# More buffers and other PSUM banks in a recurrence, one more probability buffer and sixfold softmax scalars in an attention

## The chip, the cores and the metric

The kernel runs on one core of a Trainium2 chip. Its time is the device time of one execution in microseconds (us). Five engines have an instruction stream of their own, each worked off in order: PE (TensorE, the matmuls), DVE (VectorE), ACT (ScalarE), POOL (GpSimd) and SP (SyncE, here only the issuer of DMAs). They meet through semaphores.

## The reference

A trunk of two layers on a residual stream of 1 x 1024 tokens x 1024 channels, all in float32. Each layer is a token mixer and then a gated MLP with a causal convolution.

```python
# layer 0, HGRN2, 8 heads of 128 keys and 128 values
forget = lb + (1 - lb) * sigmoid(f);  key_in = 1 - forget;  log_f = log(forget)
S_t = diag(exp(log_f_t)) S_{t-1} + k_t v_t^T;  o_t = S_t^T silu(q_t)
o = rmsnorm(o, out_norm) * silu(g);   x += o @ w_out
# layer 1, MLA, 8 heads: q and k of 128 + 64 (rotary) channels, v of 128
c_q, c_kv, k_rope = split(h @ w_in, [256, 512]);  q = rmsnorm(c_q) @ w_q_up;  k, v from rmsnorm(c_kv) @ w_kv_up
o = softmax(causal(rmsnorm(q) . rmsnorm(k) * scale)) @ v;   x += o @ w_out
# after each: conv_ffn
u = h @ w_up; y = conv3(u); gate, up = split(y); x += (silu(gate) * up) @ w_down     # width 2816
```

## The kernel before, in words

Channels lie on the partitions, tokens on the free axis, in two halves of 512 tokens (`hf`). Every float32 weight and activation of a projection is split into a high and a low part (`split`, L126 to 131: ACT casts the high part, POOL or DVE subtracts to get the low one). A product is three matmuls in the format fp32r (`acc3`, L147 to L149), and weights come 512 KB at a time by a DMA and `load_w` (tag "w", three slots). The recurrence, the transposes and the sums over tokens are plain float32 matmuls.

The kernel goes through the stages in this order: HGRN2, its output projection, FFN, MLA (its shared projections, then attention by heads), its output projection, FFN.

HGRN2 works on 16 units, a head `hd` and a half `hf` each. `project` makes F, K, q, Q, v and g of the next unit; `recur` does the recurrence of the present one. In `recur` seven score groups of 8 matmuls each (L406: once with q, then once before each of six levels) alternate with `scale`, in which DVE multiplies Q (L417) and POOL multiplies K (L419) by the products `tot` of one level. DVE puts each group into SD (L410, L429). An eighth group (`sc64`, L432) follows, ACT copies all to ST (L436 to L438), PE transposes K (`pT`, L443), ACT copies that back to K (L445), and then come for four chunks `po` (L451 and L453) and the update `pu` (L456), from which DVE or ACT makes the state (L461). `flip` transposes g (L478) and splits it, and DMAs write it away (`o_spill`); `out_projection` reads it back (`oall`).

Buffers come from pools: a tile has a tag, and the tag a number of buffers (`bufs`). In PSUM, the pool `g_ps` has two banks with tag "sc" for the score groups, sc64, pT and pu and one for po; the pool behind `ps_wo` has two banks with tag "wo" that only the first projection of the HGRN2 stage uses, and `ps_mm` has two banks for the projections. In MLA, `attend` (L694 to L757) takes for two blocks of 128 queries the scores `sp` (L710, three banks), the maximum (`mx`, `nb`), the exponential into `pp` with the sum `sm` (L725, ACT), the normalization in place (L730, ACT), transposes into `ps_wo` (L739), their split into th and tl, and the products with v (L751, L752).

The order of the instructions on each engine is not the order of the code. A scheduler puts it together while the program is built: it goes through the program with durations of its own, and picks for each engine among the instructions whose operands are ready and whose buffer is free. So a buffer more, or another bank, moves instructions far from the line that names it. On the chip the order is then fixed.

The lines that the change touches are these: the tiles Fg, K, Q and v of `project`; `sc` in `scores`, SD, tot and ST in `recur`; `mstage`; the pool `m_p` of MLA; mx, nb and sm in `attend`; and the load of the first half of the query weights, `wq`, before the first `clora`.

Of the kernel before, what the change touches and what calls it, by code (L numbers as in the profile page):

```python
# [9 lines left out]
F32 = mybir.dt.float32  # L10
# [9 lines left out]
P = 128  # L20
D = 1024
S = 1024
HF = 512
# [7 lines left out]
LEVELS = (1, 2, 4, 8, 16, 32)  # L31
# [27 lines left out]
def trunk_kernel(ctx: ExitStack, tc: tile.TileContext, x, pos, par, gout, cst, msk, w_hin, w_hout,  # L59
# [261 lines left out]
    def hgrn(layer, h):  # L321
        with ExitStack() as st:
# [28 lines left out]
            def project(hd, hf, bank=ps_mm):  # L351
                wf, wq, vgh, vgl = wts[hd]
                hh, hl, rb, y = h[hf]

                def proj(w):
                    p = bank()
                    acc3(p, [(w[0][:, k * P:(k + 1) * P], w[1][:, k * P:(k + 1) * P], hh[:, k, :], hl[:, k, :])
                             for k in range(KD)])
                    return p

                pf = proj(wf)
                Fg = early.tile([P, HF], F32, tag="F", name="Fg")
                K = tp.tile([P, HF], F32, tag="K", name="K")
                dve.tensor_tensor(out=Fg, in0=pf, in1=rb, op=ALU.mult)
                act.activation(out=K, in_=Fg, func=AF.Sigmoid, scale=-1.0)
                act.activation(out=Fg, in_=Fg, func=AF.Sigmoid)
                pool.tensor_scalar(out=Fg, in0=Fg, scalar1=oml[:, hd:hd + 1], scalar2=lb[:, hd:hd + 1],
                                   op0=ALU.mult, op1=ALU.add)
                pool.tensor_scalar(out=K, in0=K, scalar1=oml[:, hd:hd + 1], scalar2=0.0, op0=ALU.mult, op1=ALU.add)
                pq = proj(wq)  # L370
                q = early.tile([P, HF], F32, tag="q", name="q", bufs=1)
                Q = tp.tile([P, HF], F32, tag="Q", name="Q")
                dve.tensor_tensor(out=q, in0=pq, in1=rb, op=ALU.mult)  # L373
                act.activation(out=Q, in_=q, func=AF.Sigmoid)
                dve.tensor_tensor(out=q, in0=q, in1=Q, op=ALU.mult)
                dve.tensor_tensor(out=Q, in0=q, in1=Fg, op=ALU.mult)

                v = tp.tile([P, 4, P], F32, tag="v", name="v")
                g = tp.tile([P, 4, P], F32, tag="g", name="g", bufs=3)
                for tt in range(2):  # L380
                    pv = ps_mm()
                    for t2 in range(2):
                        t = 2 * tt + t2
                        ts_ = slice(t * P, (t + 1) * P)
                        acc3(pv[:, t2 * 256:(t2 + 1) * 256],
                             [(hh[:, k, ts_], hl[:, k, ts_], vgh[:, k, :], vgl[:, k, :]) for k in range(KD)])
                    p3 = v3(pv, 2)
                    for t2 in range(2):
                        t = 2 * tt + t2
                        yt = y[:, t:t + 1]  # L390
                        act.activation(out=v[:, t, :], in_=p3[:, t2, 0:P], func=AF.Identity, scale=yt)
                        act.activation(out=g[:, t, :], in_=p3[:, t2, P:2 * P], func=AF.Sigmoid, scale=yt)
                        dve.scalar_tensor_tensor(out=g[:, t, :], in0=p3[:, t2, P:2 * P], scalar=yt, in1=g[:, t, :],  # L393
                                                 op0=ALU.mult, op1=ALU.mult)
                pool.tensor_tensor(out=g, in0=g, in1=goutb[:, None, :].broadcast_to([P, 4, P]), op=ALU.mult)
                return Fg, K, q, Q, v, g

            def recur(hd, hf, prj, state):
                Fg, K, q, Q, v, g = prj

                def scores(qq):
                    sc = ps.tile([P, 4, 64], F32, tag="sc", name="sc", bufs=2)
                    for c in range(4):
                        for b in range(2):
                            sl = slice(c * P + b * 64, c * P + b * 64 + 64)
                            pe.matmul(sc[b * 64:b * 64 + 64, c, :], lhsT=K[:, sl], rhs=qq[:, sl], start=True, stop=True)  # L406
                    return sc

                SD = tp.tile([P, 4, 64], F32, tag="SD", name="SD", bufs=1)
                dve.tensor_tensor(out=SD, in0=scores(q), in1=fold[:, None, 0:64].broadcast_to([P, 4, 64]), op=ALU.mult)  # L410

                def scale(tot, m):
                    nb = HF // (2 * m)
                    tv = tot.rearrange("p (b two) -> p b two", two=2)
                    Qv = Q.rearrange("p (b two m) -> p b two m", two=2, m=m)
                    Kv = K.rearrange("p (b two m) -> p b two m", two=2, m=m)
                    dve.tensor_tensor(out=Qv[:, :, 1, :], in0=Qv[:, :, 1, :],  # L417
                                      in1=tv[:, :, 0:1].broadcast_to([P, nb, m]), op=ALU.mult)
                    pool.tensor_tensor(out=Kv[:, :, 0, :], in0=Kv[:, :, 0, :],  # L419
                                       in1=tv[:, :, 1:2].broadcast_to([P, nb, m]), op=ALU.mult)  # L420
                    nt = tp.tile([P, nb], F32, tag=f"tot{m}", name=f"tot{m}", bufs=2 if m == 64 else 1)
                    dve.tensor_tensor(out=nt, in0=tv[:, :, 0], in1=tv[:, :, 1], op=ALU.mult)
                    return nt

                tot = Fg
# [5 lines left out]
                for c in range(4):  # L431
                    pe.matmul(sc[0:64, c, :], lhsT=K[:, c * P:c * P + 64], rhs=Q[:, c * P + 64:(c + 1) * P],  # L432
                              start=True, stop=True)
                ST = tp.tile([P, 4, P], F32, tag="ST", name="ST", bufs=1)
                pool.memset(ST[64:P, :, 0:64], 0.0)
                act.copy(out=ST[0:64, :, 0:64], in_=SD[0:64])  # L436
                act.copy(out=ST[64:P, :, 64:P], in_=SD[64:P])
# [55 lines left out]
            goutb = wv.tile([P, P], F32, tag="goutb", name="goutb")  # L493
            nc.sync.dma_start(out=goutb, in_=gout.partition_broadcast(P))
            nc.sync.dma_start(out=cs, in_=cst)
            mstage = tp.tile([P, len(LEVELS), 64], F32, tag="ST", name="mstage", bufs=1)
            nc.sync.dma_start(out=mstage, in_=msk)
            dve.tensor_copy(out=masks, in_=mstage)
            prj = project(0, 0, ps_wo)
# [41 lines left out]
    def mla(h):  # L541
        with ExitStack() as st:
            tp = st.enter_context(tc.tile_pool(name="m_t", bufs=2))
            mp = st.enter_context(tc.tile_pool(name="m_c", bufs=1))
            pp_ = st.enter_context(tc.tile_pool(name="m_p", bufs=3))
            ps = st.enter_context(tc.tile_pool(name="m_ps", bufs=1, space=PSUM))
            krot = tp.tile([P, 2, HF], F32, tag="krot", name="krot", bufs=1)
            ckv = mp.tile([P, 2, 2, S], F32R, tag="ckv", name="ckv")
# [146 lines left out]
            def attend(hd, b, kk, vv, qq, rq, oh, ol):  # L695
                pts = []
                for j in (2 * b, 2 * b + 1):
# [1 line left out]
                    segs = [(0, max(w, 256))] if w <= HF else [(0, w // 2), (w // 2, w // 2)]  # L699
                    qs = slice((j % 4) * P, (j % 4 + 1) * P)  # L700
                    ns = len(segs)
                    mx = tp.tile([P, 2], F32, tag="mx", name="mx")
                    sps = []
                    for si, (c0, n) in enumerate(segs):
                        sp = ps_s()
# [7 lines left out]
                            pe.matmul(sp[:, d0:d0 + P], lhsT=identb, rhs=cmask, start=False, stop=True)  # L713
                        nv = min(n, w)
                        dve.tensor_reduce(out=mx[:, si:si + 1], in_=sp[:, 0:nv], op=ALU.max, axis=AX.X)
                    nb = tp.tile([P, 1], F32, tag="nb", name="nb")
                    if ns == 2:
                        dve.tensor_tensor(out=mx[:, 0:1], in0=mx[:, 0:1], in1=mx[:, 1:2], op=ALU.max)
                    rqj = rq[:, j % 4:j % 4 + 1]
                    dve.scalar_tensor_tensor(out=nb, in0=mx[:, 0:1], scalar=-1.0, in1=rqj, op0=ALU.mult, op1=ALU.mult)  # L720
                    pp = pp_.tile([P, S], F32, tag="p", name="pp")
                    sm = tp.tile([P, 2], F32, tag="sm", name="sm")
                    for si, (c0, n) in enumerate(segs):
                        nv = min(n, w)
                        act.activation(out=pp[:, c0:c0 + nv], in_=sps[si][:, 0:nv], func=AF.Exp, bias=nb, scale=rqj,  # L725
# [33 lines left out]

            wk = [load_w(w_min[2]), load_w(w_min[3])]  # L760
            wr = load_w(w_min[4])
            wq = [load_w(w_min[0], "wo", tp, 1)]
            raw = fetch_w(w_min[1])
            wq.append([pp_.tile([P, S], F32R, tag="p", name="wcq") for _ in range(2)])
            split(raw, *wq[1])
# [283 lines left out]
```

## Time and profile before

| what | us |
|---|---|
| median of 3 runs | 2585.41 |
| lowest and highest | 2581.57, 2588.17 |
| the profiled execution | 2581.05 |
| its span | 2579.2 |

The profiled execution stands 4.36 us under the median. The span goes from the first to the last instruction; 1.85 us lie around it. The stages, by the lines that run in them: HGRN2 up to about 545 us from the start of the span, its last unit and output projection to 650, FFN to 1351, MLA's shared projections to 1425, attention to about 1805, then the output projection and the second FFN.

The page gives for each engine the busy time, and for groups of instructions the idle time before them and which engine ended it. PE is busy in almost all of the span, so what matters is where it is idle, and what it does that is not needed.

### The profile page before, as it was taken

To read this page: it belongs to the slowest core of one execution; us is meant where nothing else is said; L and a number is where in the kernel's file an instruction comes from. 1 tells how busy PE (TensorE), PEld (TensorE's weight loads), DVE (VectorE), ACT (ScalarE), POOL (GpSimd) and SP (SyncE) were. 2 spreads that over 40 slices of the span, in tenths; PEclk is the share of its full clock that TensorE was granted. 3 is DMA by queue.
4 is the path that set the end of the run, shared out by engine and by line. 5 is a ranking of instruction groups with operands and counts; after the bars stand their busy time and mean duration, and the time that the engine had idled before them with its cause. 6 is when DMAs were issued, how large, how long until landed. Compare 5 with 4: busy or idle time off the path is not lost.

```text
span 2579.2 us, 35799 instructions
## 1 busy us (share of the span) xinstructions
PE 2483.0 (96%) x13860; PEld 2069.2 (80%) x13860; DVE 1698.1 (66%) x3033; ACT 1080.6 (42%) x1777; POOL 392.5 (15%) x386
## 2 busy tenths in 40 slices
PE   7999999998999999999999999999999999999999
PEld 6888888876777778888888788888877787888887
DVE  8355555555788888774535777777578888875333
ACT  5322223322444444433433566656444444443322
POOL 3334445521100000000003323221000000000000
PEclk9999999999999999999999999989999999999999
DMA  3111111343433332264331000002543333226443
GB/s 138 42 50 50 50 50 66 113 144 121 154 120 111 108 112 89 90 230 155 128 126 50 17 34 33 34 26 103 200 155 120 109 110 111 91 91 220 155 170 116
DMA packets 88298, 270.18 MB, mean 105 GB/s; under 512 B 9920, under 2 KB 10304, under 8 KB 86976
## 3 DMA queue, kind: packets, MB, share of 16 engines
q1 hardware_dynamic: 88128, 267.90, 29.5%
q8 instruction: 109, 1.79, 0.3%
q14 instruction: 61, 0.50, 0.1%
HBM read 207.04 MB, written 60.82 MB: 104 GB/s over the span
## 4 chain that ended last, share of the span: by engine, by line
PE 86%; DVE 6%; ACT 3%; DMA 3%; issue 1%; SPq 0%; ACTq 0%; DVEq 0%
PE ps_mm L251 19%; PE ps_up L251 9%; PE ps_mm L147 8%; PE ps_mm L149 8%; PE ps_mm L148 7%; PE ps_up L942 7%; PE ps_mm L942 5%; PE ps_wo L942 5%; PE ps_wo L251 3%; PE sp L710 3%; PE ps_misc L942 2%; PE sc L406 2%; PE ps_misc L167 2%; DMA open_spill<-part 1%; PE ps_wo L739 1%
## 5 line engine op out<-in xcount | busy, mean ns | idle before, releaser
L128 ACT CAST whi<-wraw 128x1024 fp32r<-128x1024 f32 (+1 forms) x328 | 321.3, 993 | 579.2 <-PE ps_misc L942 236.6
L131 DVE TENSOR_TENSOR wlo<-wraw,whi 128x1024 fp32r<-128x1024 f32 (+1 forms) x298 | 337.9, 1146 | 286.3 <-ACT whi L128 285.9
L251 PE MATMUL ps_mm<-bop,whi 128*128 128x512 f32 x1536 | 477.7, 393 | 17.3 <-ACT x L888 9.5
L251 PEld LDWEIGHTS ps_mm<-bop,whi 128*128 128x128 f32 x1536 | 285.9, 188 | 89.8 <-ACT x L888 15.4
L251 PE MATMUL ps_mm<-bop,wlo 128*128 128x512 f32 x768 | 296.4, 391 | 0.9 <-DVE wlo L131 0.9
L862 DVE SCALAR_TENSOR_TENSOR x<-x,prm,x 128x1023 f32<-128x1023 f32 (+1 forms) x176 | 223.5, 1279 | 48.9 <-ACT x L859 47.9
L251 PE MATMUL ps_up<-bop,whi 128*128 128x512 f32 x704 | 220.7, 394 | 0.9 <-ACT whi L128 0.9
L251 PEld LDWEIGHTS ps_mm<-bop,wlo 128*128 128x128 f32 x768 | 144.2, 188 | 33.6 <-DVE wlo L131 2.2
L942 PE MATMUL ps_up<-ring,whi 128*128 128x512 f32 x528 | 159.9, 389 | 0.0
L251 PEld LDWEIGHTS ps_up<-bop,whi 128*128 128x128 f32 x704 | 131.8, 188 | 33.1 <-ACT whi L128 2.6
L417 DVE TENSOR_TENSOR Q<-Q,tot 128x256 f32<-128x256 f32 x96 | 65.6, 683 | 133.2 <-PE sc L406 105.3
L147 PE MATMUL ps_mm<-vgh,hh 128*128 128x256 f32 x512 | 146.0, 285 | 5.9 <-DVE q L373 5.6
L149 PE MATMUL ps_mm<-vgh,hl 128*128 128x256 f32 x512 | 145.4, 284 | 0.0
L148 PE MATMUL ps_mm<-vgl,hh 128*128 128x256 f32 x512 | 143.8, 281 | 0.0
L859 ACT ACTIVATE x<-x,prm 128x1024 f32<-128x1024 f32 x88 | 109.3, 1243 | 70.0 <-DVE x L886 48.2
L251 PE MATMUL ps_up<-bop,wlo 128*128 128x512 f32 x352 | 138.5, 394 | 0.0
L845 DVE TENSOR_TENSOR wraw<-wraw 128x512 f32<-128x512 f32 x176 | 120.8, 686 | 2.2
L147 PE MATMUL ps_mm<-hh,whi 128*128 128x512 f32 x288 | 115.7, 402 | 2.2 <-DVE g L393 1.2
L710 PE MATMUL sp<-kk,qq 128*128 128x256 f32 (+4 forms) x480 | 109.1, 363 | 8.7 <-ACT pp L725 8.5
L942 PEld LDWEIGHTS ps_up<-ring,whi 128*128 128x128 f32 x528 | 99.2, 188 | 20.7
L149 PE MATMUL ps_mm<-hh,wlo 128*128 128x512 f32 x288 | 115.5, 401 | 0.0
L888 ACT COPY x<-ps_mm 128x512 f32<-128x512 f32 x84 | 49.1, 584 | 153.0 <-PE ps_mm L251 153.0
(296 smaller groups left out, 5544.3 us busy)
## 6 DMA issues: line engine op xcount, KB each, us to landing
wraw<-in_w_up_dram SPq DMA_DIRECT2D x104, 512.0 KB, 3.7
wraw<-in_w_down_dram SPq DMA_DIRECT2D x88, 512.0 KB, 3.5
act_spill<-x SPq DMA_DIRECT2D x44, 512.0 KB, 2.6
araw<-act_spill SPq DMA_DIRECT2D x88, 256.0 KB, 3.6
wraw<-in_w_hin_dram SPq DMA_DIRECT2D x38, 512.0 KB, 3.5
oall<-o_spill SPq DMA_DIRECT2D x64, 256.0 KB, 4.6
o_spill<-oh SPq DMA_DIRECT2D x32, 256.0 KB, 2.0
o_spill<-ol SPq DMA_DIRECT2D x32, 256.0 KB, 2.2
```

The source lines that it names most:

```text
L128: act.copy(out=hi, in_=src)
L131: lo_eng.tensor_tensor(out=lo, in0=src, in1=hi.bitcast(F32), op=ALU.subtract)
L147: pe.matmul(ps, lhsT=lh, rhs=rh, start=(i == 0), stop=False)
L148: pe.matmul(ps, lhsT=lh, rhs=rl, start=False, stop=False)
L149: pe.matmul(ps, lhsT=ll, rhs=rh, start=False, stop=(i == n - 1))
L251: pe.matmul(p, lhsT=a[l][:, ks], rhs=b[:, r, k, :], start=first and k == 0 and n == 0, stop=k == KH - 1 and n == 2, skip_group_check=not f ...
L417: dve.tensor_tensor(out=Qv[:, :, 1, :], in0=Qv[:, :, 1, :], in1=tv[:, :, 0:1].broadcast_to([P, nb, m]), op=ALU.mult)
L710: pe.matmul(sp[:, 0:n], lhsT=qq[:, a, qs], rhs=kk[:, c, cl], start=(i == 0), stop=last)
L845: dve.tensor_tensor(out=o, in0=p, in1=q, op=op)
L859: act.activation(out=y, in_=u, func=AF.Identity, scale=cw(2, ff), bias=pcol("cb", layer * 44 + ff))
L862: dve.scalar_tensor_tensor(out=y[:, i:S], in0=u[:, 0:S - i], scalar=cw(2 - i, ff), in1=y[:, i:S], op0=ALU.mult, op1=ALU.add)
L942: pe.matmul(acc[d], lhsT=w[l][:, d * P:(d + 1) * P], rhs=a[:, r], start=j == 0 and n == 0, stop=j == NFF - 1 and n == 2)
```

## The change

Of the recurrence: Fg, K, Q and v have three buffers where they had two; SD and ST have two where they had one; tot has two at every level where only the last had. The tile `sc` of the seven score groups of a unit goes from the pool `g_ps` (tag "sc", two banks, shared with sc64, pT and pu) to the pool of `ps_wo` (tag "wo", two banks). Of attention: `pp` has four buffers for three; mx, nb and sm have six for two. The weights `wq[0]` had a buffer of their own in the pool `m_t`; now they take one of the three slots of the tag "w", which wk[0], wk[1] and wr fill when it is loaded. No instruction is added and none taken away; each engine has as many as before.

```diff
@@ project
-                Fg = early.tile([P, HF], F32, tag="F", name="Fg")
-                K = tp.tile([P, HF], F32, tag="K", name="K")
+                Fg = early.tile([P, HF], F32, tag="F", name="Fg", bufs=3)
+                K = tp.tile([P, HF], F32, tag="K", name="K", bufs=3)
...
-                Q = tp.tile([P, HF], F32, tag="Q", name="Q")
+                Q = tp.tile([P, HF], F32, tag="Q", name="Q", bufs=3)
...
-                v = tp.tile([P, 4, P], F32, tag="v", name="v")
+                v = tp.tile([P, 4, P], F32, tag="v", name="v", bufs=3)
@@ recur
-                    sc = ps.tile([P, 4, 64], F32, tag="sc", name="sc", bufs=2)
+                    sc = psg.tile([P, 4, 64], F32, tag="wo", name="sc", padded_shape=[P, 8, 64])
...
-                SD = tp.tile([P, 4, 64], F32, tag="SD", name="SD", bufs=1)
+                SD = tp.tile([P, 4, 64], F32, tag="SD", name="SD", bufs=2)
...
-                    nt = tp.tile([P, nb], F32, tag=f"tot{m}", name=f"tot{m}", bufs=2 if m == 64 else 1)
+                    nt = tp.tile([P, nb], F32, tag=f"tot{m}", name=f"tot{m}", bufs=2)
...
-                ST = tp.tile([P, 4, P], F32, tag="ST", name="ST", bufs=1)
+                ST = tp.tile([P, 4, P], F32, tag="ST", name="ST", bufs=2)
@@ mla
-            pp_ = st.enter_context(tc.tile_pool(name="m_p", bufs=3))
+            pp_ = st.enter_context(tc.tile_pool(name="m_p", bufs=4))
...
-                    mx = tp.tile([P, 2], F32, tag="mx", name="mx")
+                    mx = tp.tile([P, 2], F32, tag="mx", name="mx", bufs=6)
...
-            wq = [load_w(w_min[0], "wo", tp, 1)]
+            wq = [load_w(w_min[0])]
```

What the scheduler makes of it, at three places. The first is PE at the end of a unit in HGRN2: the names with 2014 to 2056, K_1758 and Q_1790 belong to the old unit, those from 2108 on to the new one; ps_mm are projections. Before:

```order
L149 MATMUL ps_mm_2516<-vgh_2441,hl_112 128x256
L432 MATMUL sc64_2014<-Q_1790,K_1758 64x64 x4
L451 MATMUL po_2034<-v_1795,ST_2019 128x128 x2
L443 MATMUL pT_2028<-ident_85,K_1758 128x128 x4
L456 MATMUL pu_2038<-v_1795,K_1758 128x128
L456 MATMUL pu_2044<-v_1795,K_1758 128x128
L453 MATMUL po_2034<-state_2040,Q_1790 128x128
...
L406 MATMUL sc_2270<-q_2139,K_2108 64x64 x8
L406 MATMUL sc_2280<-Q_2140,K_2108 64x64 x8
L147 MATMUL ps_mm_2571<-vgh_2441,hh_111 128x256
```

After, on the same engine:

```order
L432 MATMUL sc64_2014<-Q_1790,K_1758 64x64 x4
L149 MATMUL ps_mm_2202<-vgh_1722,hl_409 128x256
...
L406 MATMUL sc_2270<-q_2139,K_2108 64x64 x8
L406 MATMUL sc_2280<-Q_2140,K_2108 64x64
L451 MATMUL po_2034<-v_1795,ST_2019 128x128
L443 MATMUL pT_2028<-ident_85,K_1758 128x128 x4
L451 MATMUL po_2034<-v_1795,ST_2019 128x128
L406 MATMUL sc_2280<-Q_2140,K_2108 64x64 x7
L147 MATMUL ps_mm_2451<-hh_111,whi_2431 128x512
...
L147 MATMUL ps_mm_2483<-hh_111,whi_2437 128x512
L456 MATMUL pu_2038<-v_1795,K_1758 128x128
L456 MATMUL pu_2044<-v_1795,K_1758 128x128
```

Ten matmuls of a projection and nine of scores of the new unit now stand between sc64 and po, and one po, seven score matmuls and 25 of projections between pT and pu, where nothing stood before.

The second place is PE where MLA's shared projections end and the first projection of attention, ps_mm_11895, begins. sp_11792 and sp_11817 are projections, ps_misc the sums over tokens (L167), the broadcasts of their roots (L199) and a rotation (L600). Before:

```order
L199 MATMUL ps_misc_11742<-dg_11739,ones_r_92 128x512 x2
L148 MATMUL sp_11817<-hl_11518,wcq_11340 128x512
...
L167 MATMUL ps_misc_11768<-ones_90,ksq_11764 128x2 x4
L149 MATMUL sp_11817<-hh_11517,wcq_11341 128x512
...
L199 MATMUL ps_misc_11866<-dg_11863,ones_r_92 128x512 x2
L199 MATMUL ps_misc_11883<-dg_11880,ones_r_92 128x512 x2
L147 MATMUL ps_mm_11895<-cq_11500,whi_11646 128x512
```

After:

```order
L600 MATMUL ps_misc_11718<-kr_11706,fold_104 128x512
L199 MATMUL ps_misc_11742<-dg_11739,ones_r_92 128x512 x2
L167 MATMUL ps_misc_11851<-ones_90,csq_11844 128x2 x4
L199 MATMUL ps_misc_11866<-dg_11863,ones_r_92 128x512 x2
L199 MATMUL ps_misc_11883<-dg_11880,ones_r_92 128x512 x2
L147 MATMUL ps_mm_11895<-cq_11500,whi_11646 128x512
```

The small matmuls that had projections between them now follow each other.

The third place is ACT in an odd head of attention: the exponential of sp_13227 (L725) and its neighbours, with the casts of transposed probabilities, th (L128). Before:

```order
L730 ACTIVATE pp_13221<-pp_13221,sm_13222 128x128
L128 CAST th_13026<-ps_wo_13021 128x512
L128 CAST th_13041<-ps_wo_13036 128x512
L128 CAST th_13056<-ps_wo_13051 128x512
L725 ACTIVATE pp_13237,sm_13238<-sp_13227,nb_13235,rq_12818 128x256
L128 CAST th_13070<-ps_wo_13066 128x384
```

After:

```order
L730 ACTIVATE pp_13221<-pp_13221,sm_13222 128x128
L725 ACTIVATE pp_13237,sm_13238<-sp_13227,nb_13235,rq_12818 128x256
L128 CAST th_13026<-ps_wo_13021 128x512
L128 CAST th_13041<-ps_wo_13036 128x512
L730 ACTIVATE pp_13237<-pp_13237,sm_13238 128x256
L128 CAST th_13056<-ps_wo_13051 128x512
```

The exponential has moved ahead of the three casts.

## Rows read from the trace of the kernel before

**Rows 1.** Busy time by stage: stretch and length, busy (instructions), PE clock, DMA share, GB/s.
```profile
50.00:545.00 495.00, 472.52 (x4262) 411.04 (x4263) 266.92 (x719) 145.41 (x390) 209.15 (x193) 1.00 0.18 62
545.00:650.00 105.00, 91.52 (x543) 71.93 (x542) 55.39 (x122) 28.66 (x53) 18.01 (x18) 0.93 0.38 130
...
1351.00:1425.00 74.00, 70.36 (x331) 56.95 (x330) 43.88 (x105) 27.70 (x43) 25.20 (x14) 1.00 0.15 48
1425.00:1805.00 380.00, 359.66 (x2152) 314.72 (x2151) 290.10 (x846) 238.44 (x512) 99.96 (x125) 0.94 0.12 41
```

**Rows 2.** Waits of PE, 50 to 545 us: total, times, longest.
```profile
PE pu L456 <- ACT K L445: 8.8, 12, 0.7
PE ps_mm L147 <- DVE q L373: 5.6, 13, 0.7
PE po L451 <- ACT ST L438: 3.6, 8, 0.5
...
PE po L453 <- DVE state L461: 1.1, 5, 0.2
```

**Rows 3.** Timeline of PE at a unit's end: start, duration, instruction, [idle before].
```profile
223.08 0.64 PE L443 MATMUL pT<-ident,K 128*128 128x128 f32 x4
224.46 0.71 PE L456 MATMUL pu<-v,K 128*128 128x128 f32 x4 [0.73 <-ACT K L445]
...
227.09 0.69 PE L406 MATMUL sc<-q,K 128*64 128x64 f32 x16
227.61 0.64 PE L406 MATMUL sc<-Q,K 128*64 128x64 f32 x16
228.90 0.38 PE L147 MATMUL ps_mm<-vgh,hh 128*128 128x256 f32 x1 [0.66 <-DVE q L373]
```

**Rows 4.** Timeline of PE around a score group inside a projection.
```profile
215.57 0.28 PE L148 MATMUL ps_mm<-vgl,hh 128*128 128x256 f32 x1
215.78 0.69 PE L406 MATMUL sc<-Q,K 128*64 128x64 f32 x16
216.39 0.39 PE L149 MATMUL ps_mm<-vgh,hl 128*128 128x256 f32 x1
216.62 0.28 PE L147 MATMUL ps_mm<-vgh,hh 128*128 128x256 f32 x1
```

**Rows 5.** Waits of PE, 545 to 650 us.
```profile
PE ps_misc L478 <- DVE g L471: 4.5, 1, 4.5
PE ps_mm L147 <- DMA oall<-o_spill: 4.3, 2, 2.2
```

**Rows 6.** Timeline of PE in MLA's shared projections.
```profile
1362.03 0.39 PE L147 MATMUL sp<-hh,whi 128*128 128x512 f32 x1
1362.26 0.39 PE L148 MATMUL sp<-hl,whi 128*128 128x512 f32 x1
...
1365.18 0.50 PE L147 MATMUL ps_mm<-hh,whi 128*128 128x512 f32 x1 [0.92 <-ACT csq L577]
...
1424.15 0.88 PE L199 MATMUL ps_misc<-dg,ones_r 128*128 128x512 f32 x2 [2.65 <-DVE dg L191]
```

**Rows 7.** Timeline of DVE at the start of MLA.
```profile
1351.95 11.88 DVE L230 SCALAR_TENSOR_TENSOR hl<-x,prm,hh 128x512 fp32r<-128x512 f32 x8
```

**Rows 8.** Waits of PE, 1425 to 1805 us.
```profile
PE sp L710 <- ACT pp L725: 8.5, 10, 1.5
```

**Rows 9.** Timeline of PE in one odd head, 1520 to 1620 us.
```profile
1541.02 1.00 PE L710 MATMUL sp<-kk,qq 128*128 128x320 f32 x5 [0.51 <-ACT pp L725]
1546.14 2.12 PE L710 MATMUL sp<-kk,qq 128*128 128x384 f32 x10 [1.52 <-ACT pp L725]
```

**Rows 10.** Timeline of POOL where a new head begins.
```profile
271.18 2.39 POOL L131 TENSOR_TENSOR vgl<-wraw,vgh 128x1024 fp32r<-128x1024 f32 x1 [3.03 <-ACT vgh L128]
...
276.69 1.34 POOL L395 TENSOR_TENSOR g<-g,goutb 128x512 f32<-128x512 f32 x1
278.41 2.38 POOL L131 TENSOR_TENSOR wlo<-wraw,whi 128x1024 fp32r<-128x1024 f32 x1 [0.37 <-ACT whi L128]
```

More of the change, by code (lines that the diff above doesn't have):

```diff
@@ L495, in hgrn @@
             nc.sync.dma_start(out=cs, in_=cst)
-            mstage = tp.tile([P, len(LEVELS), 64], F32, tag="ST", name="mstage", bufs=1)
+            mstage = tp.tile([P, len(LEVELS), 64], F32, tag="ST", name="mstage", bufs=2)
             nc.sync.dma_start(out=mstage, in_=msk)
@@ L715, in attend @@
                         dve.tensor_reduce(out=mx[:, si:si + 1], in_=sp[:, 0:nv], op=ALU.max, axis=AX.X)
-                    nb = tp.tile([P, 1], F32, tag="nb", name="nb")
+                    nb = tp.tile([P, 1], F32, tag="nb", name="nb", bufs=6)
                     if ns == 2:
@@ L721, in attend @@
                     pp = pp_.tile([P, S], F32, tag="p", name="pp")
-                    sm = tp.tile([P, 2], F32, tag="sm", name="sm")
+                    sm = tp.tile([P, 2], F32, tag="sm", name="sm", bufs=6)
                     for si, (c0, n) in enumerate(segs):
```

## The prediction, made before the changed kernel was run

> **What bounds the kernel now.** I read first the busy time by stage [rows 1]. PE is busy for 472.5 of 495 us in the steady part of HGRN2, 91.5 of 105 in its tail, 70.4 of 74 at MLA's start and 359.7 of 380 in attention. Since PE's work stays the same, a change of order can win only what PE waits, and can lose where it makes PE change its kind of matmul more often. The two FFNs and the end of MLA keep their order on PE, so I count them at nothing. Then I read, stage by stage, PE's waits by line and releaser, and single waits in the timeline.
>
> In HGRN2 four lines wait [rows 2]: pu for ACT's copy of the transposed K (8.8 us in 12 waits), the next projection for DVE's q, which frees its bank (5.6 in 13), po for ST (3.6 in 8), po for the state (1.1 in 5). Together 19.1 us in 38 waits. They have one cause, to be seen at the end of a unit [rows 3]: pT, pu, po and the next unit's first scores stand directly behind each other, and each needs the result of another engine on what came just before.
>
> A wait costs a little more than its idle time, since PE has to fill again. From 227.09 to 227.61 is the spacing of a score group, 0.52; the projection after the next group could have started at 228.13 and started at 228.90, which is 0.77, with 0.66 shown as idle: 0.11 more. The four transposes at 223.08 have 512 columns in all; I reckon them at twice a projection matmul of 512 columns, 0.46 [rows 6]. pu started 1.38 after them, so 0.92 late, with 0.73 shown as idle: 0.19 more. I take 0.16.
>
> **The change part by part: HGRN2.** More buffers for Fg, K, Q, v, SD, ST and tot add no instruction; they let the scheduler start the next unit's scores while the old one is at sc64, pT and pu. The bank move takes the score groups out of the way of sc64, pT and pu. The order shows that it happens: ten projection matmuls and nine of scores lie between sc64 and po, and 25 of projections between pT and pu. At 0.23 each [rows 6] those 25 alone are 5.8 us, against a wait of 0.73; so this wait goes, and that for ST (19 small matmuls, at least 1.15 for the ten at half of 0.23, and a score group of 0.52, against waits of 0.45). DVE forms q ahead of the products tot, well before the projection that wants the bank, so that wait goes too. All 38: 19.1 + 38 x 0.16 = 25.2 us.
>
> What comes next to be late? I followed both kinds of unit, with and without a new head, along the new order with durations of the trace, and found no wait on PE longer than a few tenths. I leave 2 us for such.
>
> The price is more changes between fp32r and float32 on PE. One stretch shows it [rows 4]: from 215.57 to 216.62 stand two projection matmuls, regularly 0.115 each (half the columns of one of 0.23), and a group of eight score matmuls, 0.52. 1.05 - 0.23 - 0.52 = 0.30 us for going out and back. In HGRN2 with its tail the new order has 185 such interruptions, the old 150: 35 x 0.30 = 10.5 us. From both sides: nothing, if the interruptions without a tiled matmul cost nothing, and 0.30 each. I take the upper end, the only one with a row, and keep the other for the range.
>
> The Trainium skill, "TensorEngine Tiling (Array Packing)", section "Key Properties", says that changing the tiling mode drains TensorE; scores are tiled 128*64 and all else 128*128. The row agrees in that the interruption by a tiled group costs 0.30; by the rule alone only the stretches of score matmuls would pay, of which the new order has 134 instead of 119, so 4.5 us and a sum lower by 6. No row here shows a 128*128 interruption without a wait in HGRN2, so I don't lower the sum.
>
> HGRN2: -25.2 + 10.5 + 2 = -13 us (from -25 to 0).
>
> **The tail.** The last transpose of g waits 4.5 us for DVE, and one of the two reads of oall waits 4.3 - 2.2 = 2.1 [rows 5]. In the new order 27 matmuls of the output projection stand between the last po and that transpose, 6.2 us; they cover the first. The last but one flip comes earlier, inside the v and g projections, so its read is no longer late. The other read (2.2) stays, since nothing is left to put in front of it. -4.5 - 2.1 - 2 x 0.16 = -7 us (from -10 to -2).
>
> **MLA's start.** wq[0] now waits for a slot of the tag that wk[0] holds, until the first projection of the second half has been through. So the nine matmuls of wq's projection that filled the gap before the fourth projection are gone (they began at 1362.03 [rows 6]). That projection needs a bank which ACT frees with csq, and this stands behind DVE's eight instructions for hl, 11.88 us from 1351.95 [rows 7]. DVE's order has no part in the change, so the fourth projection can't start before about 1365.18 either way: nine matmuls at 0.23 = 2.05 us of cover are lost, and the wait, now 0.92 idle, is about 3. The matmuls are not lost, they come later, where PE is to have work too; but there PE now has the small matmuls L600, L199 and L167 in one row, with nothing between. Each L199 needs a chain on DVE; with such a row once before, at 1424.15, PE waited 2.65 [rows 6]. I take one more of these: +2.05 + 2.5 = +4.5 us (from 0, if the later work fits in time, to 9, three such waits and more).
>
> **Attention.** PE waits 8.5 us for ACT's exponentials in 10 waits [rows 8]. In each of three odd heads stand two of them, 0.51 and 1.52 us [rows 9]. With a fourth buffer the exponential of sp_13227 is moved ahead of three casts on ACT, and so the bank of scores comes free earlier. 3 x (0.51 + 1.52 + 2 x 0.16) = 7 us go. mx, nb and sm let DVE run ahead and cost nothing: they hold one or two columns. What the moved exponential delays is th, on which the products with v wait; the products moved behind the next scores, so I count nothing for it; at worst a new wait as long as the longer one now, 1.5 us in each of the three heads, takes most of it back. -7 us (from -10, if all ten waits go, 8.5 + 10 x 0.16, to -2).
>
> **The sum.** -13 - 7 + 4.5 - 7 = -22.5 us, against the profiled 2581.05: 2558.5. The profiled execution is 4.36 below the median, so on the scale of the median 2585.4 - 22.5 = 2563 us.
>
> **Rivals.** First, the waits move instead of going: HGRN2 wins nothing. Two units in flight load DVE and POOL in bursts, and sixteen units need lose only 0.8 us each for that. For it speaks that ACT, DVE and POOL each wait for PE now and would be as short as before; against it that the new order has 1.7 us or more between producer and consumer at each of the places. -7 + 4.5 - 7 = -9.5, and with 9 at MLA's start -5: 2576 to 2580 us.
>
> Second, the clock. In attention the granted clock is 0.94 [rows 1], so 0.06 x 380 = 23 us go to the lower of two levels. If waits of PE cause that, and half of it comes back with them, attention wins 11 more: 2552 us or less. Against it: HGRN2 has more waits and is granted 1.00 [rows 1, 2]. The Trainium skill, "TensorE: Matmul & The Clock Gate", section "A second HAM failure mode: psum-queue depth-cycling", has it that frequent short idles between groups of matmuls let the clock swing; by that rule the change would win these 11 us, and HGRN2 speaks against it.
>
> Third, on the other side: POOL. Where a new head begins, POOL splits vgl twice, multiplies g and splits wlo, 2 x 2.39 + 1.34 + 2.38 = 8.5 us [rows 10]; all that now stands ahead of the K that the new unit's fourth score group reads, where before it stood behind or beside it. With three short ones of at most g's 1.34 and a cast ahead of half a split, the chain is at most 13.7 us. PE has until then 48 projection matmuls (11.0), three score groups (1.6) and the old unit's pT, pu and po (3.3: 223.08 to 227.09 without 0.73 [rows 3]): 15.9. So 2.2 us or more are left. If weights land later than they do now by more than that, because their DMAs stand in SP's queue behind those of o_spill, PE waits at all seven head boundaries. From 31 us in all it is slower than before, 4.4 us at each beyond the slack; at 5 us, 2563 + 35 = 2598 us.
>
> **How the numbers follow.** My forecast, 2550 to 2575, has 0.62. The clock or cheaper interruptions, below 2550: 0.12. The waits that move, 2576 to 2590: 0.19, of which 0.13 within 0.3% (7.8 us: about what a measurement of this kernel can tell from no change) and 0.06 faster than that. POOL: 0.07. So faster 0.80, same 0.13, slower 0.07. The range leaves out POOL, a part of the first rival's upper end, and gains of more than 44 us: 2541 to 2582.
>
> **What would show it.** PE's waits between 50 and 545 us: pu for K, po for ST and the projection for q should together be under 3 us; if they are over 10, that step is wrong. The span from the first projection to the last po should be 13 us shorter; if it is the whole 25, interruptions cost nothing. The wait of L478 should be gone. The fourth projection of MLA should wait about 3 us for csq, and the stretch to the first attention projection be 4 to 5 us longer. In odd heads the waits of 1.5 us for pp should be gone. I am wrong if PE waits for POOL's K at head boundaries, or if the clock in HGRN2 is under 1.00.

## The result: 43.9 us faster, about twice what was forecast

| | median of runs, us | lowest and highest | ratio to before, 95% interval |
|---|---|---|---|
| before | 2583.53 (4) | 2581.57, 2588.17 | |
| changed | 2539.59 (4) | 2538.59, 2546.54 | 0.9833 [0.9810, 0.9856] |
| changed, a second time | 2540.46 (4) | 2537.81, 2542.97 | 0.9831 [0.9817, 0.9846] |

The forecast was 2563, with a range from 2541 to 2582. The median lies 1.4 us under the lower end. Direction and places were right; the size was not.

The first profile of the changed kernel fell on its slowest execution (2546.54 us), so a second is put beside it. The starts of the same instructions, from the traces, say where the time went:

| from the start of the span, us | before | changed | second profile |
|---|---|---|---|
| first matmul of the first FFN (L251) | 670.58 | 640.99 | 638.47 |
| first scores of attention (L710) | 1429.93 | 1405.33 | 1400.73 |
| last scores of attention | 1807.71 | 1774.37 | 1768.51 |
| first matmul of the second FFN | 1895.54 | 1860.98 | 1855.10 |
| end | 2579.24 | 2544.76 | 2539.56 |

By the second profile the recurrence and its tail win 32.1 us; MLA's start gives back 3.3, after 0.4 won in the FFN; attention wins 10.0 between its first and last scores (a length that differs by some us from execution to execution, of which more below), and its output projection 1.2.

The busy time by stage of the changed kernel, first profile, to be held against [rows 1] (the second stretch here goes up to the first FFN at 641; in [rows 1] it ends at 650, 20.6 us ahead of it):

```profile
50.00:515.00 465.00, 462.01 (x4162) 405.28 (x4162) 259.71 (x703) 147.36 (x375) 208.10 (x192) 0.99 0.19 65
515.00:641.00 126.00, 121.61 (x738) 101.08 (x738) 75.73 (x150) 41.60 (x78) 23.44 (x19) 0.97 0.40 134
1322.00:1405.00 83.00, 77.72 (x349) 62.60 (x349) 44.40 (x111) 30.27 (x47) 26.29 (x15) 0.92 0.13 43
1405.00:1775.00 370.00, 353.78 (x2153) 310.24 (x2152) 285.84 (x847) 239.25 (x515) 97.63 (x123) 0.95 0.13 45
```

In the recurrence PE now is idle for 3 us of 465. These are all its waits from 50 us to the first FFN, with total, times and longest:

```profile
PE ps_mm L147 <- DMA oall<-o_spill: 2.7, 1, 2.7
PE ps_misc L167 <- DVE ol L131: 1.4, 1, 1.4
PE sc L406 <- DVE st_z L156: 1.1, 1, 1.1
PE sc L406 <- DVE yl L188: 1.0, 1, 1.0
PE sc L406 <- DVE Q L417: 0.4, 1, 0.4
PE ps_mm L148 <- DMA oall<-o_spill: 0.2, 1, 0.2
PE ps_mm L147 <- DVE Fg L364: 0.2, 1, 0.2
```

Of the four lines of [rows 2] none is left, and of [rows 5] the wait of L478 is gone, as is one of the two reads of oall.

The timeline of PE at a unit's end shows what takes the place of [rows 3]: small matmuls in groups between projections, and no idle time.

```profile
214.79 0.39 PE L147 MATMUL ps_mm<-hh,whi 128*128 128x512 f32 x1
215.02 0.61 PE L456 MATMUL pu<-v,K 128*128 128x128 f32 x4
215.38 0.48 PE L148 MATMUL ps_mm<-hl,whi 128*128 128x512 f32 x1
215.70 0.40 PE L149 MATMUL ps_mm<-hh,wlo 128*128 128x512 f32 x1
216.02 0.69 PE L406 MATMUL sc<-Q,K 128*64 128x64 f32 x16
216.64 0.50 PE L147 MATMUL ps_mm<-hh,whi 128*128 128x512 f32 x1
216.97 0.39 PE L148 MATMUL ps_mm<-hl,whi 128*128 128x512 f32 x1
...
219.02 0.39 PE L451 MATMUL po<-v,ST 128*128 128x128 f32 x2
219.25 0.39 PE L456 MATMUL pu<-v,K 128*128 128x128 f32 x2
219.39 0.48 PE L147 MATMUL ps_mm<-hh,whi 128*128 128x512 f32 x1
219.70 0.40 PE L148 MATMUL ps_mm<-hl,whi 128*128 128x512 f32 x1
219.94 0.39 PE L149 MATMUL ps_mm<-hh,wlo 128*128 128x512 f32 x1
```

Two prices are to be read here. A score group between projections: from 215.70 to 216.97 is 1.27; without two projection matmuls (0.23 each) and the group's 0.52 that leaves 0.29, as in [rows 4]. A group of untiled small matmuls: pu at 219.25 is followed after 0.14, where small matmuls among themselves stand 0.22 apart, and the projection matmul after it takes 0.31 instead of 0.23. What one loses the other saves: this way out and back costs nothing. That this holds for all of them is shown in the part on why the prediction was wrong.

### The profile page after: what moved, and what is told of

Its sections match the earlier page's. It is cut to its first block, busy times and chain, and to the rows that moved or that the text cites. A ratio compares the mean times of both kernels' runs of the same rounds, so it can differ in the third digit from the quotient of the medians.

```text
span 2544.8 us, 35686 instructions
## 1 busy us (share of the span) xinstructions
PE 2479.3 (97%) x13860; PEld 2073.6 (81%) x13860; DVE 1691.6 (66%) x3033; ACT 1087.7 (43%) x1777; POOL 390.5 (15%) x386
## 4 chain that ended last, share of the span: by engine, by line
PE 88%; DVE 6%; ACT 2%; DMA 2%; issue 1%; SPq 0%; POOL 0%; ACTq 0%; DVEq 0%; POOLq 0%
PE ps_mm L251 19%; PE ps_up L251 9%; PE ps_mm L147 8%; PE ps_mm L148 8%; PE ps_mm L149 8%; PE ps_up L942 7%; PE ps_mm L942 5%; PE ps_wo L942 5%; PE ps_wo L251 3%; PE sp L710 3%; PE sc L406 3%; PE ps_misc L942 2%; PE ps_misc L167 2%; DMA open_spill<-part 1%; PE ps_wo L739 1%
## 5 line engine op out<-in xcount | busy, mean ns | idle before, releaser
L128 ACT CAST whi<-wraw 128x1024 fp32r<-128x1024 f32 (+1 forms) x328 | 321.3, 993 | 575.1 <-PE ps_misc L942 238.0
L251 PE MATMUL ps_mm<-bop,whi 128*128 128x512 f32 x1536 | 477.8, 393 | 17.7 <-ACT x L888 9.5
L251 PEld LDWEIGHTS ps_mm<-bop,whi 128*128 128x128 f32 x1536 | 285.9, 188 | 90.5 <-ACT x L888 15.7
L251 PE MATMUL ps_mm<-bop,wlo 128*128 128x512 f32 x768 | 296.4, 391 | 1.2 <-DVE wlo L131 1.2
L251 PE MATMUL ps_up<-bop,whi 128*128 128x512 f32 x704 | 220.7, 394 | 0.7 <-ACT whi L128 0.6
L251 PEld LDWEIGHTS ps_mm<-bop,wlo 128*128 128x128 f32 x768 | 144.2, 188 | 33.9 <-DVE wlo L131 2.5
L251 PEld LDWEIGHTS ps_up<-bop,whi 128*128 128x128 f32 x704 | 131.8, 188 | 32.9 <-ACT whi L128 2.5
L251 PE MATMUL ps_up<-bop,wlo 128*128 128x512 f32 x352 | 138.5, 394 | 0.0
L710 PE MATMUL sp<-kk,qq 128*128 128x256 f32 (+4 forms) x480 | 112.4, 369 | 4.6 <-ACT pp L725 3.0
L419 POOL TENSOR_TENSOR K<-K,tot 128x256 f32<-128x256 f32 x96 | 78.3, 816 | 246.0 <-PE sc L406 196.8
L942 PEld LDWEIGHTS ps_up<-ring,whi 128*128 128x128 f32 x528 | 99.1, 188 | 20.5
L148 PE MATMUL ps_mm<-hl,whi 128*128 128x512 f32 x288 | 115.0, 399 | 0.0
```

What stands on the lines that cost most here:

```text
L128: act.copy(out=hi, in_=src)
L148: pe.matmul(ps, lhsT=lh, rhs=rl, start=False, stop=False)
L251: pe.matmul(p, lhsT=a[l][:, ks], rhs=b[:, r, k, :], start=first and k == 0 and n == 0, stop=k == KH - 1 and n == 2, skip_group_check=not f ...
L419: pool.tensor_tensor(out=Kv[:, :, 0, :], in0=Kv[:, :, 0, :], in1=tv[:, :, 1:2].broadcast_to([P, nb, m]), op=ALU.mult)
L710: pe.matmul(sp[:, 0:n], lhsT=qq[:, a, qs], rhs=kk[:, c, cl], start=(i == 0), stop=last)
L942: pe.matmul(acc[d], lhsT=w[l][:, d * P:(d + 1) * P], rhs=a[:, r], start=j == 0 and n == 0, stop=j == NFF - 1 and n == 2)
```

## The experiments

### The changed kernel once more, its two parts apart, and the weights elsewhere

The first run repeats the changed kernel; its result stands in the table above.

> The changed kernel once more. Theory A (the gain over the forecast is in the recurrence, where interruptions by untiled matmuls cost nothing): 2536 to 2542 us with the first 70 us at a clock like before's, and PE's last po of the recurrence 33 to 36 us earlier than before instead of the 30 of the first profile. Rival B (the gain over the forecast is chance between executions): a median of 2550 or more, 30 us or less gained.

The median is 2540.46 us, and the last po is 32.7 us earlier than before (588.41 against 621.10), just under what theory A had. The gain over the forecast is no chance of one execution. The 70 us at the start were not at a clock like before's, though: it is lower in both profiles of the changed kernel, more so in the first (the section on the hardware has it for the other kernels too).

The second has only the edits in `project`, `recur` and `mstage`, the third only those in `mla`:

> Only the part in the recurrence, attention and MLA's start as before. Theory A: all of the 30 to 36 us up to the last po, nothing after it, so 2548 to 2553 us. Rival (the parts help each other, or attention carries more of it than its 8.7 us in the first profile): gain under 25 us, over 2558.

> Only the part in MLA, the recurrence as before. Theory A: MLA's start 4 us slower, attention 9 faster, 1 at the output projection, so 5 to 8 us gained, 2576 to 2580. Rival: nothing or a loss, 2583 or more; or over 15 gained, if the clock in attention is what was won.

The recurrence alone: 2551.94 us, ratio 0.9876 [0.9860, 0.9892]; in its profile the first FFN begins 33.5 us earlier, and attention takes 381.4 us where the profile of before has 377.8. MLA alone: 2571.78, ratio 0.9953 [0.9935, 0.9971], 12.7 us won and not 5 to 8: its start is 3.5 slower, as expected, but attention is 15.1 shorter. 32.5 and 12.7 make 45.2, against 44.0 for the whole in the same series: the parts add up. Attention is worth more than its 8.7 us in the first profile.

The fourth moves wq[0] out of the weight slots:

```diff
-            wq = [load_w(w_min[0])]
+            raw = fetch_w(w_min[0])
+            wq = [[pp_.tile([P, S], F32R, tag="p", name="wcq") for _ in range(2)]]
+            split(raw, *wq[0])
```

> The changed kernel, but the weights wq[0] take two of the four buffers of the pool of probabilities, so that they need no slot of the weight tag and the filler matmuls at MLA's start are back. If the slot of wq[0] is what made MLA's start 4.3 us slower: 4 to 5 us under the run of the changed kernel, and the wait for csq 0.9 instead of 3. Rival (the row of small matmuls without fillers is due to the other buffers): no difference, within 2 us.

MLA's start is back at before's length (79.01 us), 3.6 us shorter than in the changed kernel (L710 begins 78.77 us after the last matmul of the FFN, in the changed kernel's second profile 82.33), and PE waits 0.9 for csq and 2.6 once for a L199. So the slot is the cause. The median, 2540.07, shows nothing of it: attention lost 22 us to the clock in this profile, against 17 in the other. It is run again below.

### Banks or buffers

The first of these kernels changes only the bank of `sc` (one line of the diff), the second only the buffers Fg, K, Q, v, SD, ST and tot.

> Of the change only the bank move of the score groups; all buffers as before. In the order, projection matmuls of 1.6 us or more stand behind each sc64 and each pT. Theory A (a unit's end is filled as soon as the banks are apart): most of the recurrence's 33 us, 28 or more, 2552 to 2558 us. Rival B (SD, ST, K, Q and v with their old buffers hold the next unit back): new waits for them on PE, 10 to 20 us gained, 2565 to 2575.

> Of the change only the buffers Fg, K, Q, v, SD, ST and tot; the score groups stay in the two banks with sc64, pT and pu. In the order, 8 of 16 units have nothing between pT and pu, and 7 of them still have something between sc64 and po. Theory A: half of the waits go, 12 to 20 us gained, 2565 to 2573. Rival (buffers are what counts): 25 or more, under 2560.

The bank alone: 2555.89 us, ratio 0.9885 [0.9870, 0.9900], 29.4 us won, and PE's waits between 60 and 560 us come to 1.5. The buffers alone: 2626.98 us, ratio 1.0151 [1.0125, 1.0177], 41.7 us slower. Both theories missed that; the third rival of the prediction, PE waiting for the K that POOL scales, is what happened. The four longest in total of PE's waits from 40 to 640 us in that kernel:

```profile
PE sc L406 <- POOL K L419: 14.5, 15, 1.0
PE ps_misc L478 <- DVE g L471: 9.6, 4, 4.3
PE sc L432 <- POOL K L419: 7.3, 7, 1.1
PE pu L456 <- ACT K L445: 7.1, 4, 2.2
```

PE and then POOL in one unit:

```profile
445.46 0.69 PE L406 MATMUL sc<-Q,K 128*64 128x64 f32 x16
447.17 0.69 PE L406 MATMUL sc<-Q,K 128*64 128x64 f32 x16 [1.02 <-POOL K L419]
448.87 1.12 PE L406 MATMUL sc<-Q,K 128*64 128x64 f32 x16 [1.01 <-POOL K L419]
```

```profile
446.30 0.81 POOL L419 TENSOR_TENSOR K<-K,tot 128x256 f32<-128x256 f32 x1 [2.89 <-PE sc L406]
448.01 0.80 POOL L419 TENSOR_TENSOR K<-K,tot 128x256 f32<-128x256 f32 x1 [0.90 <-PE sc L406]
```

But not for the reason that the rival gave (POOL busy with a new head's weights): POOL stands idle until the group before has read K, then takes 0.8 us, and three groups stand on PE with no projection between them, so each waits for the way from PE to POOL and back. The scheduler put the projections to either side of them: 25 of their matmuls stand in a row ahead of 445.46, and the next come at 449.92. From the first matmul to the last po PE waits 52 us (28 before the change), and this kernel loses clock besides, 0.96 over the 420 us from 100 to 520, where before has 1.00. So more buffers are no harmless addition when the order is made by a scheduler; with the banks apart they add 3 us of gain (29.4 to 32.5 by the medians, each to the runs of before beside it), by the profiles 5 up to the first FFN.

### What an interruption costs

In the four output projections of the changed kernel, the second matmul of each of 256 threes (the product of three matmuls) is cut in two halves of 256 columns, the first in float32; the second kernel also tiles it. In outline:

```diff
-  pe.matmul(p, lhsT=lh, rhs=rl, start=False, stop=False)
+  pe.matmul(p[:, 0:256], lhsT=lh.bitcast(F32), rhs=rl[:, 0:256].bitcast(F32), start=False, stop=False)   # first kernel
+  for b in range(2):                                                                                   # second kernel
+      pe.matmul(p[b * 64:b * 64 + 64, 0:256], lhsT=lh[:, b * 64:b * 64 + 64].bitcast(F32),
+                rhs=rl[:, 0:256].bitcast(F32), start=False, stop=False)
+  pe.matmul(p[:, 256:HF], lhsT=lh, rhs=rl[:, 256:HF], start=False, stop=False)                         # both
```

> The changed kernel, in whose four output projections the second matmul of each of 256 threes is cut in two pieces of 256 columns, of which the first is float32 on the whole array (128*128): 256 interruptions without tiling. By the spacings in the trace the piece takes 0.44 us and the other 0.117 where 0.227 was: +86 us. Theory A (an interruption by an untiled matmul costs nothing): 2626 us, and from the matmul before to the second after it nothing above the regular spacings. Rival (the price of 0.30 in the forecast): 77 more, 2703.

> The same with the float32 piece in two matmuls of 64 columns of weights each, tiled 128*64 as the scores: twice 0.44 and 0.117 where 0.227 was, +199 us. Theory A (the tiling costs about 0.30 for out and back): +77, 2816 us. Rival (neither costs anything, the 0.30 at scores has another cause): 2739.

They took 2614.69 and 2716.37 us (one run each), 74 and 176 above the changed kernel's 2540.46. Both expectations had the float32 piece about twice too dear, so their totals can't be compared with these; the spacings can. The timeline of PE in the first, and in the second:

```profile
578.21 0.40 PE L320 MATMUL ps_mm<-oall,whi 128*128 128x512 f32 x1
578.45 0.59 PE L321 MATMUL ps_mm<-oall,whi 128*128 128x256 f32 x2
578.69 0.47 PE L322 MATMUL ps_mm<-oall,whi 128*128 128x256 f32 x1
579.00 0.39 PE L323 MATMUL ps_mm<-oall,wlo 128*128 128x512 f32 x1
579.23 0.39 PE L320 MATMUL ps_mm<-oall,whi 128*128 128x512 f32 x1
```

```profile
604.51 0.40 PE L320 MATMUL ps_mm<-oall,whi 128*128 128x512 f32 x1
604.84 0.65 PE L322 MATMUL ps_mm<-oall,whi 128*64 128x256 f32 x4
605.42 0.39 PE L324 MATMUL ps_mm<-oall,whi 128*128 128x256 f32 x1
605.64 0.40 PE L325 MATMUL ps_mm<-oall,wlo 128*128 128x512 f32 x1
605.88 0.40 PE L320 MATMUL ps_mm<-oall,whi 128*128 128x512 f32 x1
```

A float32 matmul is two records; at 0.117 for each 256 columns the piece is 0.234. (L320 is the first matmul of a three.) From L320 to the next L320 the first kernel takes 1.02; 0.227 + 0.234 + 0.117 + 0.227 = 0.805 are regular, 0.21 is the interruption, and all of it lies after the float32 piece (0.31 instead of 0.117 from 578.69). The second takes 1.37, of which 1.039 are regular: 0.33, of which 0.10 lies ahead of the tiled piece. Over the whole runs, 74 - 256 x 0.124 = 42 us make 0.17, and 176 - 256 x 0.358 = 84 make 0.33. So "an untiled interruption costs nothing" fell as a rule: the change of format costs 0.17 to 0.21, the tiled piece 0.12 to 0.16 on top. (The tiled piece is two matmuls with weights of their own where the other is one; no run tells what of this is the tiling and what the second matmul.) The Trainium skill, "TensorEngine Tiling (Array Packing)", section "Key Properties", has it that a change of the tiling mode drains the engine; these runs agree, with 0.10 us of delay ahead of the tiled piece where the untiled has 0.01. In the recurrence the untiled interruption is free all the same, since its matmuls are small, 128 columns with weights of their own, spaced at 0.22 when in a row; the last of a row is followed after 0.14, which would hide what the format costs. That this slack is what hides it is a reading of the spacings, not tested by itself.

### Attention: which buffer

All three keep the recurrence as changed and wq[0] in a weight slot. One has nothing else, one sixfold mx, nb and sm, one the fourth buffer of pp.

> The recurrence as changed, and of MLA's part only the slot of wq[0]; three buffers of probabilities, two of each small tile. Theory A (the buffers of attention bring its 13 us, the slot costs 3.4 at MLA's start): 3 us slower than with the recurrence alone, 2555 us, attention as long as before, 378 to 381. Rival (the gain of attention is the clock of the executions, not the buffers): attention at 370 or less here too, 2545.

> The same and sixfold mx, nb and sm; three buffers of probabilities. Theory A (only the fourth buffer of probabilities matters): as the run with the slot alone, attention 378 to 381 us, 2555 us. Rival (the small tiles hold DVE back and with it the banks of the scores): attention 5 us shorter or more, 2550 or less.

> The changed kernel without the sixfold mx, nb and sm: the fourth buffer of probabilities alone in attention. Theory A: as the changed kernel, attention 363 to 370 us with 15 or 16 of waits and 12 to 19 lost to the clock, 2540 us. Rival (the small tiles are needed for the exponentials to move ahead): 375 or more, 2550.

| kernel | median, us | ratio to before |
|---|---|---|
| slot alone | 2554.91 | 0.9888 [0.9870, 0.9907] |
| slot and small tiles | 2555.93 | 0.9893 [0.9875, 0.9912] |
| slot and fourth pp | 2542.59 | 0.9838 [0.9816, 0.9860] |

The fourth buffer of probabilities is what counts. What it brings was split by the profiles, each from the first to the last L710: the length, PE's idle time there (all its waits added), and what the clock took (over stretches of 10 us, their length times one minus the granted clock, added up).

| attention of | length, us | waits | lost to the clock | the rest |
|---|---|---|---|---|
| before | 377.8 | 19.9 | 22.3 | 335.6 |
| bank alone | 380.8 | 19.9 | 25.7 | 335.1 |
| buffers alone | 381.0 | 18.4 | 28.3 | 334.2 |
| recurrence alone | 381.4 | 18.9 | 28.4 | 334.0 |
| slot alone | 382.4 | 21.2 | 25.8 | 335.4 |
| slot and small tiles | 384.1 | 23.8 | 25.4 | 334.9 |
| changed, first | 369.0 | 15.8 | 18.8 | 334.5 |
| changed, second | 367.8 | 15.9 | 16.9 | 335.0 |
| MLA alone | 362.7 | 14.9 | 11.7 | 336.1 |
| slot and fourth pp | 369.8 | 9.6 | 27.3 | 332.9 |

Each row is one execution. The first four rows, without an edit in MLA, have a mean of 380.3 us, the three with the whole of MLA's part 366.5: 13.8 us, of which 4 are waits (19.3 to 15.5) and 10 the clock (26.2 to 15.8). The kernel with the fourth pp alone is 10.5 under that mean in another way, 9.7 of waits and nothing of the clock. What the clock will do was not told by the waits: the kernel with the least of them lost 27 us. So what the second rival supposed, that waits of PE set the clock, isn't borne out in attention (in the recurrence of the kernel with the buffers alone, more waits and a lower clock did come together), and what sets it in attention stays open. The 10 us are uncertain too: the other kernels with a fourth buffer of probabilities lost 13.7 and 20.5 (the two with cut matmuls) and 22 and 20.3 (the two runs with wq[0] elsewhere), so with the fourth buffer it is 11.7 to 27.3, without it 22.3 to 28.4.

### A version that should be better

> The changed kernel with wq[0] in two buffers of the pool of probabilities, once more. If the 3.5 us won at MLA's start hold and attention's clock falls by chance like that of the changed kernel (12 to 19 us lost instead of 22): 2536 to 2538 us. Rival (attention's order here is the worse for the clock): 2540 again, and 20 us or more lost to the clock.

The same kernel as the fourth of the first series. Its median here is 2536.91 us (5 runs), ratio 0.9829 [0.9809, 0.9850]; attention took 369.1 us with 20.3 lost to the clock: the time is the one expected, the clock that of the rival. MLA's start was again shorter than in the second profile of the changed kernel, 78.25 us against 82.33 from the last matmul of the FFN. Over both series its nine runs have a median of 2539.56, the eight of the changed kernel 2539.81. It beats the kernel before, but from the changed one the times can't tell it.

## Why the prediction was wrong, point by point

No single step carries the miss. Of the 21 us that the forecast was short, the price of the interruptions is about 6, the size of the waits with the 2 kept back about 8, and attention, where the clock was left out, about 7. The sums here are of the spacings on PE up to the first FFN: each start minus the start before it, less the regular spacing (0.227 for 512 columns, 0.117 for 256, 0.111 for a record of a small matmul, 0.0325 for one of a score). The regular parts are the same in both kernels, 560.9 us.

| us up to the first FFN | before | changed, second profile | difference | forecast |
|---|---|---|---|---|
| at starts that waited | 43.7 | 5.7 | -37.9 | -25.2 - 7 + 2 |
| at all others (kinds that change) | 43.8 | 47.9 | +4.1 | +10.5 |
| first 67 us | 13.1 | 14.9 | +1.8 | 0 |

**The step that failed in the recurrence is the price of the interruptions.** "35 x 0.30 = 10.5 us ... I take the upper end, the only one with a row": the row was that of a tiled score group, and the change adds almost only the other kind. Interruptions that hold scores are 103 in the old order and 104 in the new; those without are 48 and 82. All that the new order adds came to 4.1 us: about 6 at the full clock, less 2 in the tail, where the kernel before ran longer at the lower clock (granted 0.93 from 545 to 650 us in [rows 1], 0.97 from 515 to 641 in the changed kernel).

The same spacings give each kind its price in the second profile, from the matmul before an interruption to the second after it, without those that waited and after the first 67 us. The 41 interruptions by pT, po and pu alone cost 0.01 us each, all 80 without scores 0.03. The 68 by scores alone cost 0.34 each; 31 more hold scores in 60 stretches, with small matmuls between, and cost 20.2 us in all, again 0.34 a stretch. So the price went by stretches of scores. The prediction counted them, 134 instead of 119, reckoned 4.5 us and set that aside; 15 at 0.34 are 5.1. Whether it is the tiling or the scores' format that a stretch pays for isn't told apart here.

Nor was "No row here shows a 128*128 interruption without a wait in HGRN2" true of the trace that the prediction had. It holds 37 of them between 67 and 545 us, at 0.06 each. In this one, from 121.05 to 121.73 is 0.68, which is two projection matmuls of 256 columns at 0.117 and four records of pu at 0.111, with nothing left over:

```profile
121.05 0.28 PE L147 MATMUL ps_mm<-vgh,hh 128*128 128x256 f32 x1
121.17 0.60 PE L456 MATMUL pu<-v,K 128*128 128x128 f32 x4
121.53 0.36 PE L148 MATMUL ps_mm<-vgl,hh 128*128 128x256 f32 x1
121.73 0.28 PE L149 MATMUL ps_mm<-vgh,hl 128*128 128x256 f32 x1
```

**What comes next to be late: nothing**, where 2 us were kept back; one wait of 0.4 is left of the recurrence after its first units. **The waits themselves** were sized 5 to 6 us too low: in the steady part 27.9 us instead of 25.2, and in the tail four small ones (2.0 together, three of them of lines of [rows 2]) and one of 1.2 for DVE's x were not counted, beside the 4.5 and 2.1 of [rows 5]. Both of these went as said. Of the signs that the prediction named, a clock under 1.00 in HGRN2 did come (0.99 from 50 to 515 us), but all of the loss lies before 67 us.

**MLA's start** came out at +3.3 us for +4.5, near by luck and not by its steps. The wait for csq was to grow to 3 us. It is gone: DVE needs 7.61 us for the eight hl and not the 11.88 of [rows 7], so the prediction's "can't start before about 1365.18 either way" failed. In its place the row of small matmuls without fillers has two waits for a L199, where before had one of 2.65 and one more of 2.5 had been put:

```profile
1395.90 1.60 PE L199 MATMUL ps_misc<-dg,ones_r 128*128 128x512 f32 x2 [2.43 <-DVE dg L191]
1399.57 1.19 PE L199 MATMUL ps_misc<-dg,ones_r 128*128 128x512 f32 x2 [2.07 <-DVE dg L191]
```

Together the waits grew by only 0.9 us, from 3.6 to 4.5 in the second profile. What cost more is the clock: between the last matmul of the FFN and the first L710 it took 6.8 us there and 1.7 before, and all else is 2.7 shorter. The eight profiles with wq[0] in a weight slot have 5.1 to 6.8 lost in this stretch, the six others 0 to 4.3. The prediction had no term for that.

**Attention** was sized at -7; it was -13.8 over the profiles above. The wait of 1.52 us of [rows 9] is gone in all three odd heads, as said, and the line of [rows 8] fell from 8.5 to 3.0, while the transposes wait for pp as before (2.1 in all then, 2.2 now):

```profile
PE sp L710 <- ACT pp L725: 3.0, 7, 0.8
...
PE ps_wo L739 <- ACT pp L730: 2.2, 2, 1.8
```

Others took a part of it back, so that 4 us of waits are won. The other 10 are the clock, a term that the sum put at nothing: the second rival, worked out at 11 us and given 0.12. The size came near, but its mechanism, waits of PE that lower the clock, is not shown.

**The sum, by medians and profiles:** -32.1 in the recurrence and its tail (forecast -20), +3.3 at MLA's start, -13.8 in attention (forecast -7), about -1 in its output projection: -43.6, beside 43.9 measured.

**The rivals.** The first did not come. The third came not in the changed kernel, where no start waits for POOL's K, but in the one with the buffers alone.

## What to carry to other kernels

Take the price of an interruption from a row of the same kind: here 0.3 us for a stretch of tiled scores, 0.2 for a long float32 matmul and nothing for a row of small ones, and the forecast put one price on all. Where a scheduler makes the order, more buffers and more banks are different things and have to be tried apart: the bank alone won 29 us, the buffers alone lost 42, and both together won 32. A stage's time has three parts, work, waits and the granted clock, and it pays to add up all three before a gain is put down to the waits.

## What the runs showed of the hardware that was not expected

**An instruction of DVE takes four times as long beside a split on POOL.** DVE's eight hl at MLA's start take this in the changed kernel, and POOL's instructions beside it are these:

```profile
1323.07 7.61 DVE L230 SCALAR_TENSOR_TENSOR hl<-x,prm,hh 128x512 fp32r<-128x512 f32 x8
```

```profile
1323.75 2.40 POOL L131 TENSOR_TENSOR wlo<-wraw,whi 128x1024 fp32r<-128x1024 f32 x1 [3.41 <-ACT whi L128]
1330.73 2.43 POOL L131 TENSOR_TENSOR wcq<-wraw,wcq 128x1024 fp32r<-128x1024 f32 x1 [4.58 <-ACT wcq L128]
```

One split lies beside the eight, and one of the eight takes 2.97 us where the seven others take about 0.74. In the kernel before three splits lie beside them:

```profile
1352.65 5.81 POOL L131 TENSOR_TENSOR wlo<-wraw,whi 128x1024 fp32r<-128x1024 f32 x2 [3.42 <-ACT whi L128]
1360.22 2.40 POOL L131 TENSOR_TENSOR wcq<-wraw,wcq 128x1024 fp32r<-128x1024 f32 x1 [1.76 <-ACT wcq L128]
```

There three of the eight take 2.90 to 2.91 us, and all eight 11.88. With the recurrence alone and with wq[0] elsewhere it is the same, 11.85 and 11.88: 4.3 us more for two more splits. In the changed kernel the split of wq[0] is gone from here, since its load waits for a slot, and that of wcq starts just behind the eight.

**The clock at the start.** In the first 100 us the clock took 1.7 us in the profile of before and 6.8, 5.1, 3.4 and 5.1 in those of the changed kernel (first, second), of the recurrence alone and of the bank alone. It falls where PE waits between the first units, at about 50 to 65 us. The new order is not shown to be the reason: of the kernels with the same recurrence, the one with the slot alone lost 6.8 there, and that with small tiles and the second run with wq[0] elsewhere 1.7, as before.
